# The framework's timeline scheduler in place of its default for a two-block stack on one core

## The chip, the cores and the metric

The kernel runs on one core of a Trainium2 chip. The metric is the device time of one execution in microseconds; the median of three runs of the kernel before is 1540.05 us (1540.02 to 1541.18).

The engines are named as in the profile: PE multiplies matrices (PEld is its weight load), DVE is the vector engine, ACT the scalar engine, POOL the general one, and SP issues the transfers (SPq is its queue). Each takes its instructions in the order of its own list and waits at an instruction until the operands are there.

## The reference

256 tokens of width 1024 pass through two blocks. All matrices are float32 in HBM. The first block has two layers, each a mixer and an MLP with modulated norms; the second has three mixers side by side, a cross attention to 256 memory tokens and a gated feed-forward:

```python
for layer in range(2):                                   # first_block
    sh1, sc1, g1, sh2, sc2, g2 = split(silu(c) @ ada_w[layer] + ada_b[layer], 6)
    h = rmsnorm(x, norm_g[layer, 0]) * (1 + sc1) + sh1
    mixed = ssd_na_mixer(h, ...) if layer == 0 else mlstm_mixer(h, ...)
    x = x + g1 * rmsnorm(mixed, norm_g[layer, 1])
    h = rmsnorm(x, norm_g[layer, 2]) * (1 + sc2) + sh2
    x = x + g2 * rmsnorm(square(relu(h @ mlp_w1[layer])) @ mlp_w2[layer], norm_g[layer, 3])

fq, fk, fv, ff, su, hq, hf, hi, hg, gl = split(rmsnorm(x, norm_mix) @ w_in)   # second_block
gates = sigmoid(gl)
merged = (gates[0] * (fox_attention(fq, fk, fv, ff) @ wb[0])
          + gates[1] * (s5_mixer(su) @ wb[1])            # scan, gelu, then gated by z @ w_glu
          + gates[2] * (hgrn2_mixer(hq, hf, hi, hg) @ wb[2]))
x = x + merged @ w_out
x = x + cross_attention(rmsnorm(x), rmsnorm(mem), ...)
x = x + swiglu(rmsnorm(x), w_gate_up, w_down)
```

`ssd_na_mixer` is a two-way state-space scan (SSD) and a neighbourhood attention of 16 heads, joined by one output matrix.

## The kernel before

The weights are streamed from HBM in units of 1 MB: `unit` (L431) loads one into a tile `raw` (3 buffers), ACT rounds each half to a high part `wh` (L351), and DVE subtracts it for the low part `wl` (L360); there are 4 buffers of each, so two units at a time. Every product is three matmuls on high and low parts (L366). A projection unit is 48 matmuls with 256 columns, one of an output matrix 24 with 512. Transposes run on PE as well (L370). PSUM has eight banks, shared between the tags `mm` (projections) and `ax` (all else), four and four, five and three in the second block's mixer.

`stack_kernel` (L1863) writes the stages one after the other. The stretches of the trace are: the start, to 44 us, where the modulation vectors are made on DVE from 1 MB units of `ada` (L635) while the first tokens are normed; the projections of `mixer0`, 44 to 218; its eight output units and what goes with them, 218 to 283; the norm into the first MLP, to 295; first MLP, mLSTM mixer, second MLP, to 950; `mixer2`, 950 to 1280; `cross`, to 1345; `ffn`, to the end.

In `mixer0` (L968) M0_ORDER, "aaaxxxaaaxbzaaazaaazz", gives the order of 21 steps: `a` projects queries, keys or values of four heads, `x` and `z` belong to the scan. After every third `a` the heads of a column c are queued as a generator (`na_heads`), which makes two pairs of heads, each with its bias tables `nb` (L1100): scores into `ax`, a reduction on DVE that adds the table (L1109, `nam`), exponentials on ACT, transposes on PE, and the product with the values from the tile `smp`. `tick` runs a step of a queued generator between the units. `out_units` then sums eight output units in four accumulators (here `mm_2649` to `mm_2652`), in the order of M0_ROWS, the four of the attention first.

Into the MLP, `mem_fill` puts projections of the memory (`mm_3127`, `mm_3186`, in fwh and fwl tiles) where PE would wait for the norm; `order` (L885) asks that the first of them be issued ahead of the norm's transposes.

In `mixer2` (L1650) M2_ORDER, "su fox hz hv g2 g0 b0 glu dr g1 b1 b2", names projections, gates (`g`), branch products (`b`) and the S5 gate (`glu`); the S5 scan (tiles s5w, su, s5c) is a background generator and the HGRN scan (xn, hS, hb) a queued one, in levels: xn on DVE, products on PE, a predicated copy into hS on DVE (L1513).

The code so far gives an order of creation and the data dependencies. The framework's scheduler makes the list of each engine from it: it simulates the program and puts next what it takes for ready. The first argument of `TileContext` is the device; the mode of that simulation is an option of it.

## Time and profile before

| | before |
|---|---|
| median of the runs | 1540.05 us |
| profiled execution | 1534.84 us |
| its span | 1533.0 us |
| mean granted clock of PE | 0.991 |
| PE busy | 1472.9 us (96%) |
| DVE busy | 1164.9 us (76%) |
| ACT busy | 854.5 us (56%) |

The rows further down come from this one execution, whose time is its span and 1.8 us around it. PE's matmuls overlap in the records: one is shown with 0.28 us where the next starts 0.12 us later, so the pace is read from rows that group many of them.

### The profile page before, as it was taken

How to read it: one execution, taken by the hardware profiler on the slowest of the kernel's cores; microseconds unless marked ns; L12 is line 12 of the kernel's file. 1: busy time of each engine (PE TensorE's matmuls, PEld its weight loads, DVE VectorE, ACT ScalarE, POOL GpSimd, SP SyncE). 2: the span in 40 equal slices, each digit the busy share in tenths (PEclk: the TensorE clock that was granted, in tenths of full speed). 3: DMA queues.
4: the chain of work that ended last, by engine and by line, in shares of the span. 5: the costliest groups of instructions: out<-in, count | busy, mean ns of one | idle time of the engine just before them, and what ended most of it. 6: DMA issues, size and time to landing. Idle time of an engine off the chain costs nothing.

```text
span 1533.0 us, 25395 instructions
## 1 busy us (share of the span) xinstructions
PE 1472.9 (96%) x9964; PEld 1318.1 (86%) x9964; DVE 1164.9 (76%) x2223; ACT 854.5 (56%) x1502; POOL 4.5 (0%) x24
## 2 busy tenths in 40 slices
PE   2998999999999899999999999999999999999999
PEld 2887887888988899998889889877789998799998
DVE  7788988877778886657988866867798987565555
ACT  4786774654456555545756765445444457444443
POOL 0000000000000000000000000000000000000000
PEclk8999999999999999999999999999999999999999
DMA  9755887587875894446676664323333365245542
GB/s 347 258 166 171 293 300 275 185 308 289 319 296 187 300 297 152 166 145 221 232 246 242 232 226 187 133 95 131 130 132 135 114 227 199 97 141 189 193 178 98
DMA packets 62058, 315.47 MB, mean 206 GB/s; under 512 B 6385, under 2 KB 15217, under 8 KB 28146
## 3 DMA queue, kind: packets, MB, share of 16 engines
q1 hardware_dynamic: 61938, 313.85, 57.6%
q8 instruction: 78, 1.28, 0.3%
q14 instruction: 42, 0.34, 0.1%
HBM read 304.77 MB, written 9.05 MB: 205 GB/s over the span
## 4 chain that ended last, share of the span: by engine, by line
PE 77%; DVE 12%; DMA 5%; ACT 5%; issue 2%; SPq 0%; ACTq 0%; DVEq 0%
PE mm L366 50%; PE ax L366 24%; DVE wl L360 3%; PE ax L370 2%; DMA bp<-cs_d 1%; ACT xn L351 1%; ACT wh L351 1%; DMA raw<-in_ada 1%; DVE acc L751 1%; ACT nb L351 1%; DMA grow<-in_rows 1%; DVE acc L638 1%; DMA raw<-in_wts 1%; DMA bp<-nM_d 1%; PE mm L370 0%
## 5 line engine op out<-in xcount | busy, mean ns | idle before, releaser
L360 DVE TENSOR_TENSOR wl<-raw,wh 128x1024 fp32r<-128x1024 f32 x400 | 485.9, 1223 | 204.6 <-ACT wh L351 203.2
L351 ACT ACTIVATE wh<-raw 128x1024 fp32r<-128x1024 f32 x400 | 419.4, 1057 | 372.0 <-PE mm L366 212.2
L366 PE MATMUL mm<-xh,wh 128*128 128x256 f32 x1536 | 441.4, 287 | 6.1 <-ACT bp L351 3.1
L366 PE MATMUL mm<-xh,wl 128*128 128x256 f32 x1536 | 439.3, 286 | 2.5 <-DVE wl L360 2.5
L366 PE MATMUL mm<-xl,wh 128*128 128x256 f32 x1536 | 438.8, 286 | 0.0
L366 PEld LDWEIGHTS mm<-xh,wh 128*128 128x128 f32 x1536 | 295.9, 193 | 15.2 <-issue 5.6
L366 PEld LDWEIGHTS mm<-xh,wl 128*128 128x128 f32 x1536 | 295.9, 193 | 7.5 <-DVE wl L360 3.7
L366 PEld LDWEIGHTS mm<-xl,wh 128*128 128x128 f32 x1536 | 296.0, 193 | 5.6 <-issue 3.8
L366 PE MATMUL mm<-wh,xh 128*128 128x256 f32 x496 | 143.9, 290 | 0.0
L366 PE MATMUL mm<-wl,xh 128*128 128x256 f32 x496 | 143.2, 289 | 0.5 <-DVE wl L360 0.5
L366 PE MATMUL mm<-wh,xl 128*128 128x256 f32 x496 | 142.0, 286 | 0.0
L366 PE MATMUL ax<-wh,mhh 128*128 128x512 f32 x256 | 102.5, 400 | 0.0
L366 PE MATMUL ax<-wh,mhl 128*128 128x512 f32 x256 | 101.4, 396 | 0.0
L366 PE MATMUL ax<-wl,mhh 128*128 128x512 f32 x256 | 101.4, 396 | 0.0
L366 PEld LDWEIGHTS mm<-wl,xh 128*128 128x128 f32 x496 | 96.0, 194 | 4.9 <-issue 2.3
L366 PEld LDWEIGHTS mm<-wh,xh 128*128 128x128 f32 x496 | 95.8, 193 | 2.2 <-issue 1.7
L366 PEld LDWEIGHTS mm<-wh,xl 128*128 128x128 f32 x496 | 95.9, 193 | 1.2 <-issue 1.1
L366 PEld LDWEIGHTS ax<-wh,mhl 128*128 128x128 f32 x256 | 48.2, 188 | 11.9 <-DVE mhl L360 0.4
L366 PEld LDWEIGHTS ax<-wh,mhh 128*128 128x128 f32 x256 | 48.3, 189 | 10.6 <-ACT wh L351 0.5
L366 PEld LDWEIGHTS ax<-wl,mhh 128*128 128x128 f32 x256 | 48.2, 188 | 10.6 <-issue 0.2
L751 DVE CUSTOM_DVE_ANT_0 acc<-raw,crow 128x1024 f32<-128x1024 f32 x32 | 39.0, 1219 | 3.0 <-DMA raw<-in_ada 2.7
L363 DVE SCALAR_TENSOR_TENSOR acc<-raw,cond,acc 128x1024 f32<-128x1024 f32 x28 | 35.8, 1278 | 6.5 <-DMA raw<-in_ada 6.2
(486 smaller groups left out, 2574.5 us busy)
## 6 DMA issues: line engine op xcount, KB each, us to landing
raw<-in_wts SPq DMA_DIRECT2D x214, 1024.0 KB, 4.9
raw<-in_ada SPq DMA_DIRECT2D x48, 1024.0 KB, 5.8
nb<-in_nab SPq DMA_DIRECT2D x16, 256.0 KB, 5.0
grow<-in_rows SPq DMA_DIRECT2D x16, 256.0 KB, 6.1
bp<-cs_d SPq DMA_DIRECT2D x16, 256.0 KB, 5.5
s5tab<-s5t SPq DMA_DIRECT2D x16, 256.0 KB, 2.7
s5tl<-s5tab SPq DMA_DIRECT2D x16, 256.0 KB, 3.6
meml<-mem_d SPq DMA_DIRECT2D x2, 1024.0 KB, 5.3
```

The source lines that it names most:

```text
L351: return self.nc.scalar.activation(out=out, in_=in_, func=func, **kw)
L360: return self.nc.vector.tensor_tensor(out=out, in0=in0, in1=in1, op=op)
L363: return self.nc.vector.scalar_tensor_tensor(out=out, in0=in0, scalar=s, in1=in1, op0=op0, op1=op1)
L366: return self.nc.tensor.matmul(out, lhsT, rhs, start=start, stop=stop)
L370: return self.nc.tensor.transpose(out, in_, self.ident[0:k, 0:k])
L638: nc.vector.tensor_tensor_reduce(out=acc, in0=raw[:, k * D:(k + 1) * D], in1=self.crow, scale=1.0, scalar=0.0, op0=ALU.mult, op1=ALU.add, ...
L751: nc.vector.tensor_tensor_reduce(out=acc, in0=w, in1=self.crow, scale=1.0, scalar=0.0, op0=ALU.mult, op1=ALU.add, accum_out=s8[:, j:j + 1])
```

## The change

The scheduler is asked for its other mode, which keeps a timeline of the engines while it chooses. Nothing else is edited; every engine has the same instructions as before (9,528 matmuls, 2,223 rows on DVE, 1,366 activations, 400 transfers), and POOL has them in the same order.

```diff
-    with tile.TileContext(nc) as tc:
+    with tile.TileContext(nc, schedule_with_timeline_sim=True) as tc:
         stack_kernel(tc, aps)
```

On SP, at the start of the program, right after the first tokens (raw from in_ada are modulation units, nf a small weight, cst masks, nb attention tables, mem the memory tokens, raw from in_wts weight units; + is the place after the change):

```order
 L635 DMA raw_196<-in_ada 128x2048
+L461 DMA nf_244<-in_wsm 128x512
+L1878 DMA cst_80<-in_cst 128x512
+L1100 DMA nb_689<-in_nab 128x512
+L1100 DMA nb_692<-in_nab 128x512
+L1100 DMA nb_822<-in_nab 128x512
+L978 DMA crow_d_90<-G0_86 1x1024
+L1100 DMA nb_825<-in_nab 128x512
+L847 DMA mem_1674<-in_mem 128x1024
 L635 DMA raw_201<-in_ada 128x2048
 L438 DMA raw_222<-in_wts 128x2048
 L438 DMA raw_232<-in_wts 128x2048
```

Eight small transfers moved ahead of the second modulation unit; two tiles of gain rows, grow, moved in the same way, behind raw_289.

On PE, a pair of attention heads in `mixer0`; before, next to projections (ax_2385 is the product with the values, ax_2434 and ax_2437 the scores of the following pair, mm_2464 a projection):

```order
L366 MATMUL mm_2464<-xl_109,wh_2467 128x256
L366 MATMUL ax_2385<-smp_2426,nv_2381 64x256
L366 MATMUL ax_2385<-smp_2410,nv_2381 64x256
L366 MATMUL ax_2385<-smp_2426,nv_2381 64x256
L366 MATMUL ax_2385<-smp_2410,nv_2381 64x256
L366 MATMUL ax_2437<-nk_2312,nq_2244 128x256
L366 MATMUL ax_2434<-nk_2312,nq_2244 128x256
L366 MATMUL ax_2437<-nk_2312,nq_2244 128x256
L366 MATMUL ax_2434<-nk_2312,nq_2244 128x256
L366 MATMUL mm_2464<-xh_108,wl_2468 128x256
```

And on PE now, behind all projections, the pair before those two (ax_2016 the product with the values, ax_2065 and ax_2068 its scores and their transposes):

```order
L366 MATMUL ax_2068<-nk_1872,nq_1735 128x256
L366 MATMUL ax_2065<-nk_1872,nq_1735 128x256
L366 MATMUL ax_2068<-nk_1872,nq_1735 128x256
L366 MATMUL ax_2065<-nk_1872,nq_1735 128x256
L366 MATMUL ax_2391<-nk_2312,nq_2244 128x256 x2
L370 MATMUL ax_2065<-cst_80,nb_2063 128x128 x4
L370 MATMUL ax_2068<-cst_80,nb_2066 128x128 x4
L366 MATMUL ax_2388<-nk_2312,nq_2244 128x256 x2
L366 MATMUL ax_2016<-smp_2173,nv_2012 64x256
L366 MATMUL ax_2016<-smp_2087,nv_2012 64x256
L366 MATMUL ax_2016<-smp_2173,nv_2012 64x256
L366 MATMUL ax_2016<-smp_2087,nv_2012 64x256
```

The last four of the eight pairs moved behind the last projection, among the output units, and between the scores of this one and its product stand only the scores of the next.

On DVE, in `mixer2` between the splits of two gate units, before (wl_12932 and wl_12936 are one unit, wl_12993 the first half of the next):

```order
L360 TENSOR_TENSOR wl_12932<-raw_12929,wh_12931 128x1024
L360 TENSOR_TENSOR wl_12936<-raw_12929,wh_12935 128x1024
L357 TENSOR_SCALAR s5w1_12524<-s5w1_12524 128x512
L360 TENSOR_TENSOR xn_12763<-xn_12763,hq_10267 128x64x8
L360 TENSOR_TENSOR s5w1_12524<-s5w1_12524,su0_10329 128x512
L360 TENSOR_TENSOR wl_12993<-raw_12990,wh_12992 128x1024
```

And now, the last twelve of the 64 rows from wl_12936 to wl_12993 (s5c_12523 is the operand of the glu product):

```order
L360 TENSOR_TENSOR su1_10390<-su1_10390,s5w2_12533 128x512
L360 TENSOR_TENSOR xn_12797<-xn_12797,hq_10267 128x256x2
L360 TENSOR_TENSOR s5c_12523<-su1_10390,s5bt_12522 128x512
L1513 COPY_PREDICATED hS0_12255<-G0_86,ax_12802 128x512
L1513 COPY_PREDICATED hS1_12257<-G0_86,ax_12808 128x512
L360 TENSOR_TENSOR xn_12814<-hb_12172,hz_10266 128x512
L360 TENSOR_TENSOR xn_12814<-hb_12172 128x512
L360 TENSOR_TENSOR xn_12814<-xn_12814,hq_10267 128x512
L357 TENSOR_SCALAR s5w1_12524<-s5w1_12524 128x512
L360 TENSOR_TENSOR s5w1_12524<-s5w1_12524,su0_10329 128x512
L1513 COPY_PREDICATED hS0_12255<-G0_86,ax_12819 128x512
L360 TENSOR_TENSOR wl_12993<-raw_12990,wh_12992 128x1024
```

Three rows stood between these two units, 62 stand there now: the end of the S5 scan and six levels of the HGRN scan, which were spread over the units before.

Into the first MLP, PE's list before has the four groups of transposes of the norm at the start of mm_3186 and behind its 18th and 25th matmul (two, one, one); now all 48 matmuls of mm_3186 come first and the four groups behind them.

## Rows read from the trace of the kernel before

**Rows 1.** The page: busy time of an engine; the chain that ended last.
```profile
PE 1472.9 (96%) x9964; PEld 1318.1 (86%) x9964; DVE 1164.9 (76%) x2223; ACT 854.5 (56%) x1502; POOL 4.5 (0%) x24
...
PE 77%; DVE 12%; DMA 5%; ACT 5%; issue 2%; SPq 0%; ACTq 0%; DVEq 0%
```

**Rows 2.** Windows: stretch, length, busy time (instructions) by engine, clock, DMA share, GB/s.
```profile
44.00:218.00 174.00, 161.75 (x1228) 142.96 (x1227) 148.33 (x349) 129.20 (x289) 0.00 (x0) 0.97 0.70 232
218.00:283.00 65.00, 64.55 (x328) 52.69 (x325) 56.83 (x98) 35.59 (x58) 0.00 (x0) 1.00 0.74 268
...
950.00:1174.00 224.00, 222.15 (x1497) 181.14 (x1496) 176.86 (x341) 100.75 (x168) 1.08 (x2) 1.00 0.37 128
1174.00:1224.00 50.00, 49.46 (x416) 48.86 (x416) 46.51 (x80) 25.89 (x34) 0.00 (x0) 1.00 0.36 127
```

**Rows 3.** Timeline of SP's queue: start, length, what is issued.
```profile
4.62 6.66 SPq L635 DMA_DIRECT2D raw<-in_ada  x2
13.48 7.08 SPq L438 DMA_DIRECT2D raw<-in_wts  x2
```

**Rows 4.** Windows of the start, and the sizes of transfers in the first 50 us.
```profile
2.00:18.00 16.00, 2.02 (x10) 1.97 (x11) 10.87 (x43) 6.49 (x17) 0.00 (x0) 1.00 1.02 392
...
20.00:22.00 2.00, 0.00 (x0) 0.00 (x0) 1.66 (x7) 2.00 (x5) 0.00 (x0) 1.00 0.43 74
...
nb<-in_nab SPq DMA_DIRECT2D x4, 256.0 KB, 6.1
mem<-in_mem SPq DMA_DIRECT2D x1, 512.0 KB
```

**Rows 5.** Timeline of DVE, end of the start: start, length, operation, idle before.
```profile
43.97 2.36 DVE L360 TENSOR_TENSOR wl<-raw,wh 128x1024 fp32r<-128x1024 f32 x2 [0.26 <-ACT wh L351]
```

**Rows 6.** Timelines of PE and DVE: one pair of attention heads, and the next.
```profile
148.76 0.38 PE L366 MATMUL ax<-nk,nq 64*128 64x256 f32 x1
...
156.05 1.08 PE L366 MATMUL ax<-smp,nv 128*64 128x256 f32 x8
...
149.50 0.42 DVE L1109 CUSTOM_DVE_ANT_0 nb<-ax,nb 128x256 f32<-128x256 f32 x1
...
158.99 0.41 DVE L1109 CUSTOM_DVE_ANT_0 nb<-ax,nb 128x256 f32<-128x256 f32 x1
```

**Rows 7.** The chain that ended last, in the first MLP: start, length, what.
```profile
307.14 5.60 PE ax L366 x24
313.18 5.75 PE mm L366 x48
```

**Rows 8.** Timeline of PE at a stall, and windows behind it.
```profile
122.66 1.97 PE L366 MATMUL ax<-qt,xt 128*64 128x256 f32 x8 [4.09 <-DVE qt L360]
...
122.00:124.00 2.00, 1.34 (x8) 0.77 (x8) 1.74 (x2) 0.52 (x1) 0.00 (x0) 0.50 0.54 103
...
126.00:128.00 2.00, 2.00 (x11) 2.00 (x11) 1.15 (x4) 0.10 (x1) 0.00 (x0) 0.50 0.44 175
```

**Rows 9.** Timeline of PE into the first MLP: last transposes, first projection that waited.
```profile
290.22 0.65 PE L370 MATMUL mm<-cst,xn 128*128 128x128 f32 x4
...
295.00 0.39 PE L366 MATMUL mm<-xh,wh 128*128 128x256 f32 x1 [1.14 <-ACT wh L351]
```

**Rows 10.** The second block's mixer: timeline of PE at mm_12633; two pieces of the chain.
```profile
1174.31 0.37 PE L366 MATMUL mm<-fyh,wh 128*128 128x256 f32 x1
...
1163.19 3.63 PE ax L366 x24
...
1198.64 1.90 PE mm L366 x16
```

**Rows 11.** The same mixer: timeline of DVE, rows of the HGRN scan.
```profile
1189.06 0.72 DVE L1513 COPY_PREDICATED hS<-G,ax 128x512 f32<-128x512 int32 x1
1189.68 0.68 DVE L360 TENSOR_TENSOR xn<-hb,hz 128x512 f32<-128x512 f32 x1
1190.28 0.69 DVE L360 TENSOR_TENSOR xn<-hb 128x512 f32<-128x512 f32 x1
```

## The prediction

> **What bounds the kernel now.** I read the page first, then the busy time by stage, then the timeline where a stage is not full of TensorE work. The page shows PE busy for 96% of the span and PE on 77% of the chain that ended last [rows 1]: the kernel is as long as PE's work plus the moments in which PE has nothing to do. The stages differ. From 44 to 218 us (the 22 projections of the first mixer) PE is busy 161.75 of 174 us while DVE is busy 148.33; from 1174 to 1224 PE is busy 49.46 of 50 and DVE 46.51; from 950 to 1174 PE is busy 222.15 of 224 [rows 2]. So an order that keeps all the work can gain at most the idle time (12.25 us in the first mixer, some 13 us of DMA-bound start, next to nothing later), while it can lose wherever DVE, which has 3.5 us of air in 50 around 1200 us, is given its work at the wrong time. The question for each stage is whether PE still finds ready operands.
>
> **The change, place by place.** The instructions are the same on every engine; each engine works through its list in order, so work that another engine's list has put late is late for PE too. I compared the two lists and gave each row the duration that the trace of before has for the same instruction; "so much less done" below is the sum of the rows that the new list has moved behind a point. The MLPs, the mLSTM mixer, the cross attention and the feed-forward keep their order of weight units, or move rows by a few us where PE is full; I take them as nothing, and 1 us each way in the range.
>
> *Start.* The first 44 us wait for DMA: from 2 to 18 us the queue moves 392 GB/s, about 0.4 MB a us, and only at 20 to 22 us does it fall to 74 GB/s [rows 4], where it waits for a raw buffer. The new list of SP puts nf, cst, crow, four neighbourhood tables (256 KB each) and the 512 KB of mem ahead of the second of the two modulation units that before went out together at 4.62 us [rows 3, 4]. Of that, nf, cst and crow came before the first projection unit anyway; what is new ahead of it is the four tables, mem and two tiles of gain rows (grow), 1.0 + 0.5 + 0.5 = 2.0 MB, or 5 us at 0.4 MB a us. The hole at 20 to 22 us can take back some 1.5 us of it. The first split of a weight unit for the projections, at 43.97 us [rows 5], would come 3.5 us later; PE's later waits in the mixer may hide a little of this. I take +3, bounds 0 (all hidden) and +5 (no hole filled).
>
> *First mixer, projections.* The new order runs more projections before the first attention and splits weight units earlier on DVE; by the last projection DVE has done 11 us less, ACT 22 us less and PE 10 us less than before, all of it attention and scan work put behind. PE waits less for splits as long as that lasts: of the 12.25 us idle I take two thirds back, -8, bounds 0 and -12.
>
> *First mixer, tail.* What was put behind comes due with the eight out-projection units. Before, the last of the eight pairs of attention heads is done inside the last projection; now four pairs stand behind it, and from the third out unit on the matmuls need their results. One pair is a chain over PE, DVE and ACT: its scores are on PE at 148.76 us, DVE reads them at 149.50, the product with the values runs at 156.05 to 157.13 us, and the next pair's DVE part starts at 158.99 [rows 6]. From scores to product it is 8.4 us and from pair to pair 9.5. In the new PE list the first of the four pairs has one out unit of 24 matmuls (5.60 us [rows 7]) between scores and product, the second only the next pair's scores, the third 24 matmuls again, the fourth a handful of normalisation matmuls, some 1.5 us. Four chains of 8.4 us are 33.6; scores of the third run beside the second, about 2.5 us off; cover 5.6 + 5.6 + 1.5 = 12.7. PE waits 33.6 - 2.5 - 12.7 = 18 us. Softmax work of different pairs may overlap more than I see, so I take +15, bounds +8 (only the second and fourth wait, 4 us each) and +22 (9.5 us a pair, less overlap).
>
> *Into the first MLP.* Before, 30 of the 48 matmuls of the second memory filler stand between groups of transposes of the normed tokens, and 23 stand behind the last group; with them in place PE still waits 1.14 us for the first projection [rows 9]. Now all 48 come first and all four groups of transposes follow, with nothing behind. 48 matmuls take 5.75 us [rows 7], so 23 are 2.8 us of cover gone, and the 1.14 stays: +3, bounds +1 (the transposes start sooner) and +4. The same pattern is at the end of the second MLP, with fewer matmuls: +1.
>
> *The mixer of the second block.* Here the list of DVE puts the end of the S5 scan and six levels of the HGRN scan behind the unit splits of the branch and gate projections. Up to the projection mm_12633, which started at 1174.31 us, DVE has 32 us less done, PE 48 matmuls of the scans less. 24 of such matmuls take 3.63 us [rows 10], so PE comes there 7.3 us earlier, at 1167, and is through with it and its twin, 48 matmuls, at 1172.8. But DVE's row merged3 waits for that, and behind it, before the second half of the glu operand (s5c from su1), now stand 52 rows of the scans, and the split wl_12993 some nine rows later. On this stretch a row follows the one before every 0.60 to 0.63 us [rows 11]; a fifth of the 52 rows are shorter ones, so 52 rows are about 31 us without any wait, 36 with the busy times instead of the spacing. The operand is there at 1204 to 1209. PE's list still has 34 glu matmuls, 33 of mm_12928 and 16 small ones in front of mm_12989, about 10 us, which therefore starts at 1214 to 1219 instead of 1198.64 plus some tenths, where the rows of before have it [rows 10]. That is 15 to 20 us. After it both lists have the same work left and DVE is lighter, but PE was full there before, so nothing comes back. I take +14, since PE can spread some of the waiting matmuls; bounds +5 and +20.
>
> **A clock cost on top.** In this trace PE sat idle for 4.09 us ahead of 122.66 us, and from 122 to 128 us it ran at a granted clock of 0.50, 1.2 GHz instead of 2.4 [rows 8]: a long stall is followed by some us at half speed, and a matmul of 1.2 GHz takes twice its time, so a stall costs up to 3 us more than its length. I count it in the range, not in the sum, since most matmuls right behind these stalls are followed by another wait. The Trainium skill, TensorE: Matmul & The Clock Gate, section Loop structure matters more than you think, says the same as a rule: matmuls have to stay back to back, and a long wait makes the array run cold. Rows 8 agree; by that rule the sum would be some 6 us higher.
>
> **The sum.** Against the profiled execution of 1534.84 us (span 1533.0): start +3, projections -8, tail +15, norm gaps +3 and +1, second mixer +14, together +28, or 1563. The median of the runs is 1540.05, 5.2 us or 0.34% above the profiled one; on that scale 1563 is 1568.
>
> **Rivals.**
> - *The stalls come, with the clock behind them.* Each of the four pair waits and the wait for s5c is followed by half speed, and the bounds at the upper end hold: 1568 + 6 for the clock + 7 for the tail + 6 for the mixer, 1575 to 1587. For it: rows 8. Against: the cover in the tail gets slower too and then hides nothing that is lost.
> - *The early splits win.* This ends on the other side, faster. The place is the projections of the first mixer: if DVE, busy 148.33 of 174 us, is what keeps PE waiting there, the whole 12 us come back; if the four pairs then overlap so far that only 4 us of wait is left in the tail, and DVE's 52 rows in the second mixer start before merged3's wait is over, so that 2 us are lost, the sum is 3 - 12 + 4 + 1 + 2 = -2, or -6 with the start and the norm gap hidden: 1534 to 1538. It decides by whether the pair-to-pair time without projections around it falls below 5 us; the 8.4 us within a pair speak against, as do the rows in order on DVE.
> - *No difference.* The same work on a PE that is 96% busy, gains at the projections equal to the losses: 1540, when the tail costs 8 and the mixer 1. The point is the same as above.
> - *PE is not really full.* The weight loads (PEld) are busy 181.14 of 224 us where PE is busy 222.15 [rows 2]. If that difference were air, a better order could press up to a fifth out of this stretch, and with 13 us of it the time would be 1555. The Trainium skill, Perfetto Trace Analysis, section Identifying the Most-Contended Engine, holds matmul busy time for a poor measure and weight-load time for a better one. Against: where PE does nothing but back-to-back matmuls of one form, it keeps their pace, 5.75 us for 48 [rows 7], and there too weight loads are not all of it; so I give it 3 in 100.
>
> **How the numbers follow.** Forecast near 1568 (1555 to 1575) 52 in 100; stalls with the clock (1575 to 1592) 20; a smaller loss (1544 to 1555, among it the fourth rival), 10; no difference 6; faster 12. The likeliest gives 1568. The range must hold 8 in 10: from 1546, which leaves out the two cases at or under 1543 (18 in 100), up to 1592. A measurement of this kernel can tell about 0.2%, 3 us, from no change; by the cases, slower 0.82, within it 0.06, faster 0.12.
>
> **What would show it.** In the new profile: the first split of a projection unit after 46 us instead of 43.97 (start); PE's busy share from there to the last projection over 0.93 (projections); PE waits of several us for nb or smp among the out units, and that stage over 75 us instead of 65 (tail); a wait for wh or xh of 3 to 5 us at the first matmul of the first MLP; in the second block a wait of PE of 10 us or more for s5c with DVE busy without a break. The prediction is wrong if the out units run without waits, which means that a pair is no chain of 8.4 us when alone, or if the glu matmuls find s5c ready, which means that DVE went through the scan rows before the PE work that I took to hold it.

## The result, and the profile after

The changed kernel takes 1606.87 us (median of 4 runs, 1605.35 to 1609.24), the kernel before 1540.32 on the same chip: a ratio of 1.043, 95% interval 1.041 to 1.045. It is slower, as forecast, but by 66.5 us and not by 28: beyond the upper end of the range. The profiled execution took 1606.95 us, with a span of 1605.2 instead of 1533.0.

The page of the changed kernel answers to [rows 1]: first the busy time of the engines, then the engines' shares of the chain that ended last.

```profile
PE 1499.5 (93%) x9964; PEld 1339.2 (83%) x9964; DVE 1161.5 (72%) x2223; ACT 853.2 (53%) x1502; POOL 4.5 (0%) x24
...
PE 77%; DVE 9%; DMA 8%; ACT 4%; issue 2%; SPq 0%; ACTq 0%; DVEq 0%
```

DVE and ACT are busy 3.4 and 1.3 us less than before. PE has the same 9,964 records, and they took 26.6 us more; the other 45.6 us of the 72.2 are idle time of PE. So two things cost: PE waits more, and its matmuls take longer.

To see where, I cut both traces at the same matmuls, those with which a stage begins. The cuts are at 54.80 and 297.30 us in the changed kernel where they are at 50.20 and 279.60 in the one before, and so on. A stretch then has nearly the same work in both; only 20 records have passed from the mLSTM mixer to its output units. Windows of the kernel before (stretch, length, busy us and records of PE, PEld, DVE, ACT and POOL, granted clock, DMA share, GB/s), for the first mixer, the norm into the first MLP, the mLSTM mixer's output units with the norm into the second MLP, and the second block's mixer:

```profile
50.20:279.60 229.40, 216.71 (x1471) 186.05 (x1471) 198.57 (x427) 159.59 (x338) 0.00 (x0) 0.98 0.70 235
279.60:318.80 39.20, 37.72 (x290) 36.04 (x289) 32.27 (x77) 25.58 (x55) 0.00 (x0) 1.00 0.57 209
...
645.60:761.20 115.60, 113.91 (x718) 102.54 (x717) 86.54 (x211) 66.53 (x133) 0.53 (x1) 1.00 0.53 191
...
937.50:1247.20 309.70, 307.31 (x2207) 265.61 (x2206) 249.02 (x451) 144.81 (x222) 2.07 (x4) 1.00 0.38 134
```

The same four of the changed kernel, and behind them the cross attention:

```profile
54.80:297.30 242.50, 222.61 (x1471) 187.98 (x1471) 194.53 (x415) 157.43 (x334) 0.00 (x0) 0.94 0.65 219
297.30:342.70 45.40, 40.49 (x289) 38.23 (x288) 33.81 (x88) 27.04 (x59) 0.00 (x0) 0.92 0.47 169
...
671.00:801.60 130.60, 121.58 (x738) 108.68 (x737) 93.83 (x237) 72.57 (x148) 0.53 (x1) 0.96 0.48 170
...
981.00:1308.40 327.40, 313.22 (x2207) 271.15 (x2206) 249.42 (x450) 143.31 (x220) 2.07 (x4) 0.97 0.37 128
1308.40:1424.00 115.60, 105.77 (x607) 92.50 (x607) 72.13 (x173) 62.00 (x136) 0.00 (x0) 0.96 0.43 157
```

In the first mixer the same 1,471 records of PE took 5.9 us longer, and PE's idle time (length less busy time) rose from 12.7 to 19.9 us; the two make up the 13.1 us. All stretches, read in the same way:

| stretch of the kernel before, us | longer by | forecast | PE idle before, after |
|---|---|---|---|
| start, to 50.2 | +4.6 | +3 | 28.9, 31.7 |
| first mixer, to 279.6 (projections −15.6, output units +28.7) | +13.1 | +7 | 12.7, 19.9 |
| into the first MLP, to 318.8 | +6.2 | +3 | 1.5, 4.9 |
| first MLP, to 469.2 | 0.0 | 0 | 0, 0 |
| its norm and the mLSTM mixer, to 645.6 | +1.5 | 0 | 6.1, 9.2 |
| output units of that mixer, into the second MLP, to 761.2 | +15.0 | 0 | 1.7, 9.0 |
| second MLP, to 937.5 | +3.1 | +1 | 1.0, 3.2 |
| second block's mixer, to its first output unit, 1247.2 | +17.7 | +14 | 2.4, 14.2 |
| its output units, cross attention, to 1351.8 | +11.0 | 0 | 2.1, 9.8 |
| feed-forward, to the end | 0.0 | 0 | 3.7, 3.8 |

The stretches in which weights stream through a full PE, the first MLP and the feed-forward, are as long as before to a tenth of a us. All that was lost stands in the mixers and at the places where one stage hands over to the next.

**The start.** The timeline of DVE has the first split of a projection unit at 47.81 us, against 43.97 [rows 5]:

```profile
47.81 2.36 DVE L360 TENSOR_TENSOR wl<-raw,wh 128x1024 fp32r<-128x1024 f32 x2 [0.26 <-PE mm L366]
```

**The first mixer's output units.** The timeline of PE (start, length, operation, idle before and what ended it) and two windows show the pairs of heads that were put off, to be held against the pair in [rows 6]:

```profile
231.24 0.84 PE L370 MATMUL ax<-cst,nb 128*128 128x128 f32 x4 [0.97 <-ACT nb L351]
233.94 1.12 PE L370 MATMUL ax<-cst,nb 128*128 128x128 f32 x4 [1.85 <-ACT nb L351]
235.74 1.98 PE L366 MATMUL ax<-smp,nv 128*64 128x256 f32 x8 [0.69 <-ACT smp L351]
242.76 1.92 PE L370 MATMUL ax<-cst,nb 128*128 128x128 f32 x8 [2.05 <-ACT nb L351]
246.61 1.98 PE L366 MATMUL ax<-smp,nv 128*64 128x256 f32 x8
258.16 1.08 PE L366 MATMUL ax<-smp,nv 128*64 128x256 f32 x8
267.45 1.08 PE L366 MATMUL ax<-smp,nv 128*64 128x256 f32 x8
...
235.00:240.00 5.00, 4.32 (x19) 2.72 (x19) 0.23 (x1) 0.60 (x1) 0.00 (x0) 0.51 1.01 408
...
245.00:250.00 5.00, 3.87 (x14) 1.83 (x13) 1.80 (x10) 3.12 (x12) 0.00 (x0) 0.50 0.28 101
```

The waits are for exponentials (`nb`) and for normalised products (`smp`), as the forecast said, but none is longer than 2.05 us. Behind them the granted clock is 0.50, 1.2 GHz, and the product of 8 matmuls takes 1.98 us instead of 1.08 [rows 6]. The four products follow one another after 10.9, 11.5 and 9.3 us, against 9.5 from pair to pair in the kernel before.

**The second block's mixer.** The chain that ended last (start, length, what) behind the row `merged3`, shortened to where engines change:

```profile
1208.26 0.60 DVE merged L363
1208.85 1.20 DVE s5w L360 x2
...
1214.31 5.48 PE ax L366 x16
1219.81 0.73 DVE hS L1513
1220.54 1.17 DVE xn L360 x2
...
1230.07 5.51 PE ax L366 x24
1235.60 0.73 DVE hS L1513
1236.33 1.17 DVE xn L360 x2
...
1238.85 2.74 PE ax L366 x16
```

It is DVE's block of scan rows that the forecast saw, but it doesn't run through: every level of the HGRN scan needs matmuls that stand alone on PE, and these run slowly, 24 in 5.51 us where [rows 10] has 24 in 3.63. The window around the first of them:

```profile
1210.00:1215.00 5.00, 2.74 (x10) 2.14 (x11) 5.00 (x11) 0.00 (x0) 0.00 (x0) 0.50 0.43 180
```

DVE is busy for the whole of it, PE for half, at the lower of its two clocks.

**A place the forecast had passed over: how a stage ends.** In the kernel before the last two output units of a stage run the first 128 tokens and then the other 128, so two of the four accumulators are whole some 7 us ahead of the others, and the norm's first half is hidden. First before, then after, ACT's first read of the accumulators behind the mLSTM mixer:

```profile
715.26 0.60 ACT L351 ACTIVATE xn<-mm 128x512 f32<-128x512 f32 x1 [0.93 <-PE mm L366]
...
751.27 0.60 ACT L351 ACTIVATE xn<-mm 128x512 f32<-128x512 f32 x1 [0.43 <-PE mm L366]
```

Before, these units go on for another 6.5 us behind 715.26, to 721.8. After, the second half can be read 1.15 us behind the first (at 752.42), so nothing covers the norm, and PE waits. The memory filler that was meant to cover it needs a PSUM bank which the norm still has to empty. Its first matmul in the changed kernel, here and at the end of the first MLP:

```profile
509.35 0.46 PE L366 MATMUL ax<-fwh,memh 128*128 128x256 f32 x1 [4.41 <-DVE x L363]
...
757.40 0.55 PE L366 MATMUL mm<-fwh,memh 128*128 128x256 f32 x1 [5.47 <-DVE x L363]
```

The six stages end in the kernel before with 6.8 to 7.0 us between the first and the last accumulator; in the changed one with 0.7 to 2.8.

### The profile page after: what moved, and what is told of

It is laid out like the page before. It is cut to its first block, busy times and chain, and to the rows that moved or that the text cites. A ratio compares the mean times of both kernels' runs of the same rounds, so it can differ in the third digit from the quotient of the medians.

```text
span 1605.2 us, 25434 instructions
## 1 busy us (share of the span) xinstructions
PE 1499.5 (93%) x9964; PEld 1339.2 (83%) x9964; DVE 1161.5 (72%) x2223; ACT 853.2 (53%) x1502; POOL 4.5 (0%) x24
## 4 chain that ended last, share of the span: by engine, by line
PE 77%; DVE 9%; DMA 8%; ACT 4%; issue 2%; SPq 0%; ACTq 0%; DVEq 0%
PE mm L366 51%; PE ax L366 24%; DMA raw<-in_wts 5%; DVE wl L360 2%; ACT wh L351 2%; PE ax L370 2%; DMA raw<-in_ada 1%; DVE fwl L360 1%; ACT nb L351 1%; DMA bp<-nM_d 1%; DMA bp<-cs_d 1%; DVE acc L638 0%; DMA grow<-in_rows 0%; DVE acc L751 0%; ACT nf L351 0%
## 5 line engine op out<-in xcount | busy, mean ns | idle before, releaser
L366 PEld LDWEIGHTS mm<-xh,wl 128*128 128x128 f32 x1536 | 297.7, 194 | 14.2 <-DVE wl L360 8.0
L366 PEld LDWEIGHTS ax<-wh,mhh 128*128 128x128 f32 x256 | 48.7, 190 | 13.2 <-ACT mhh L351 2.4
L351 ACT ACTIVATE xn<-xn 128x128 f32<-128x128 f32 (+3 forms) x44 | 24.6, 577 | 35.2 <-DVE xn L360 27.2
```

Of the source, the lines that this page charges most:

```text
L351: return self.nc.scalar.activation(out=out, in_=in_, func=func, **kw)
L366: return self.nc.tensor.matmul(out, lhsT, rhs, start=start, stop=stop)
```

## The experiments

Three theories stood against one another: that the lost stagger of the accumulators makes the loss (S); that displaced scan, attention and norm work does, each at its own place (D); and, later, that the order of the transfers does (T). The figures in brackets are ratios to the kernel before with their 95% intervals. The us that came "back" are differences between medians of four occasions, on which the kernel before had 1540.32, 1539.82, 1538.96 and 1538.08 us, so they are good to about 2 us. Changes of a stage are read at the cuts of the table, in one profiled execution of each kernel.

**e1, the stagger given back.** The changed kernel; only in a stage's last units the second half's matmuls are asked to come behind the first half's:

```diff
         for t in range(2):
-            for i, (_, yh, yl) in enumerate(units):
-                self.down_half(...)
+            with self.tc.issue_after(self.last_pe.ins) if t and last else nullcontext():
+                for i, (_, yh, yl) in enumerate(units):
+                    self.down_half(...)
```

> The changed kernel, with one thing put back: in the last output units of every stage the matmuls of the second token half are issued behind those of the first, so that the accumulators of tokens 0 to 127 end some 6 us ahead of the others, as before the change. Theory S (the part of the loss that the forecast missed lies at the stage boundaries, where the four accumulators now end within 1 to 3 us of each other and the norm and the fillers have nothing to run beside): 25 to 35 us of the 66 come back, 1572 to 1582 us, and the gaps ahead of the first filler out of the mLSTM mixer (5.5 us) and into the MLPs close. Theory D (the loss is all in work put off inside the two large mixers): 0 to 6 us, 1601 to 1607.

Measured 1598.46 us (1.038, 1.035 to 1.040): 8.4 us back, between the two. In the profiled execution, 4.5 us faster than that median, the way into the first MLP gained 3.1 us on the changed kernel, the end of the mLSTM mixer 1.5, the way out of the second MLP 2.1, and the cross attention with the end of the mixer before it 6.8. The chain behind the mLSTM mixer shows why it is so little:

```profile
748.35 0.70 ACT xn L351 x2
...
751.24 0.68 DVE x L363
752.05 8.49 PE mm L366 x48
```

The first half is read earlier, but the rows of the norm still come one behind the other on ACT and DVE, and PE stands for 3.74 us ahead of 752.05. The edit is not the stagger alone, either: the scheduler simulates anew, and inside the mLSTM mixer all three engines' lists are no longer those of the changed kernel.

**e2, the stagger taken from the kernel before.**

```diff
+            for part in (0, 1) if last else ((0, 1),):
+                for t in range(2):
+                    self.down_half(ws[i], yh, yl, acc, t, f, l, part)
```

> The kernel before, default scheduler, with one thing taken over: the matmuls of a stage's last output units go through both token halves in turn, so that all four accumulators end together. Theory S: 20 to 35 us slower, 1560 to 1575. Theory D: within 5 us of before, 1540 to 1545.

Measured 1561.46 us (1.014, 1.011 to 1.017): 21.6 us lost, as theory S expected, 3.6 on average at each of six ends. In the profile the loss stands behind the ends: 2.5, 2.7, 4.0 and 5.1 us behind the first four, 7.1 behind the last two together. The timeline of PE shows the same wait as in the changed kernel, at a place where the kernel before has none:

```profile
732.25 0.58 PE L366 MATMUL mm<-fwh,memh 128*128 128x256 f32 x1 [3.39 <-DVE x L363]
```

So in the kernel before the stagger is worth as much as a third of the loss, and giving it back on one engine isn't enough. That the norm's rows on the others have to be in step with it fits e1's chain; no run changes those rows alone.

**e5, e6 and e8, one mixer each in its order of before.** These are the changed kernel with one stage (its norm included) held to the order of before on PE, DVE and ACT. The same edit stands around `mixer2` (e5), `mixer0` (e6) and `mixer1`, the mLSTM mixer (e8):

```diff
+def as_listed(tc, rows):
+    made = {i.name: i for i in rows}
+    for names in ROWS:                      # the list of before, an engine at a time
+        last = None
+        for n in names:
+            i = made.get(n)
+            if i is not None:
+                if last is not None:
+                    tc.add_manual_dep(i, last.name, NOSYNC, reason="listed order")
+                last = i
...
+    lo0 = len(tc.nc.cur_bb.bb.instructions)
     with S.phase("mixer2", 5, LATE2):
...
+    as_listed(tc, list(tc.nc.cur_bb.bb.instructions)[lo0:])
```

> The changed kernel, but all that is created in the second block's mixer and its norm (PE, DVE, ACT) is issued in the order of the kernel before, by order-only dependencies; the rest stays with the timeline scheduler. From the two traces this stage with the step into the next cost 18 us in the mixer and 5 at its exit. Theory D: 15 to 25 us come back, 1582 to 1592, and the glu product no longer waits for s5c. Rival (its loss is a loss of PE clock and transfers around it, which stay): under 6 us, 1601 to 1607.

Measured 1586.63 us (1.031, 1.029 to 1.033): 20.2 us back, within the range of theory D. The stage is 4.5 us longer than before instead of 17.7, and the block of scan rows is gone. That is 13.2 us in place; another 5.3 came back in the norm and the mLSTM mixer, whose lists the edit leaves as they were. The same lists took 177.9 us there in the changed kernel, 176.3 in e4, 180.5 in e6 and 172.6 in e5, where the clock was 1.00 instead of 0.97. So the figure of a stage from one execution can move by several us without any edit to it, and in place the edit gave less than the 15 us expected. The stretch in which the changed kernel had the chain above is now:

```profile
1214.00:1240.00 26.00, 26.00 (x222) 25.87 (x222) 25.27 (x38) 14.35 (x20) 0.00 (x0) 1.00 0.32 111
```

PE is full at a clock of 1.00 beside a full DVE.

> The changed kernel, but all that is created in the first mixer and its norm (PE, DVE, ACT) is issued in the order of the kernel before. From the two traces the projections gained 16 us, the out units lost 29 and the step into the first MLP 6. Theory D (gain and loss are one thing, attention put off): both go, net 15 to 20 us come back, 1587 to 1592. Rival (the projections' gain is a thing of its own): the projections gain stays in the rest and only the transfers change, under 6 us.

Measured 1593.88 us (1.034, 1.032 to 1.037): 13.0 us back, 2 short of what theory D expected. From the first projection to the last the stage is 0.6 us longer than before and its output units 0.7, instead of −15.6 and +28.7: the gain and the loss go together. The windows' row of the output units has 1.1 us of idle time left:

```profile
224.40:284.00 59.60, 58.50 (x280) 46.86 (x280) 51.92 (x78) 33.60 (x50) 0.00 (x0) 1.00 0.72 264
```

> The changed kernel, but all that is created in the mLSTM mixer and its norm is issued in the order of the kernel before (PE, DVE, ACT). From the two traces its out units with the step into the second MLP cost 10.4 us and the MLP's first units 4.5; with the accumulators alone put back (e1) 1.8 of the 10.4 came back. Theory D (the heads of this mixer are put off too, so that the last out units wait for them): the out units are back to before, 9 to 14 us less, 1593 to 1598. Rival (the accumulators' common end is all of it): 2 to 4 us less, 1603 to 1605.

Measured 1599.72 us (1.039, 1.037 to 1.042): 7.2 us back, between the two theories. In place it is clear, the output units of the mLSTM mixer lose 0.0 us instead of 10; but from the end of the first MLP to these units the trace is now 7.3 us longer than before instead of 1.5, and the second MLP's beginning is still 4.0 late. Of the 7.3, 3.4 stand at the step out of the first MLP, which the edit leaves in the new order, and 3.9 in the beginning of the listed mixer; why those is not shown.

**e9, all three mixers and the cross attention.** The same edit around all of them.

> The changed kernel, with the three mixers and the cross attention in the order of before on PE, DVE and ACT; the start, both MLPs and the feed-forward stay as the timeline scheduler has them. If the parts add up: 72 us of the trace less 13 (first mixer), 6 and 5 (the steps around it), 14 (mLSTM mixer and its exit), 18 and 11 (second mixer to feed-forward) leaves 5 to 10, 1545 to 1550. If the parts only shift waits to other places: 1560 or more.

Measured 1563.92 us (1.016, 1.013 to 1.019): 43.0 us back. The three alone gave 20.2, 13.0 and 7.2, together 40.4, but here the cross attention is listed too, and in the profile its stretch is 1.5 us longer than before instead of 11.0. So the whole is some 7 us less than the sum of its parts. The time is above what was expected if the parts add up, and in the range of the rival: what is left, 25 us, is the start (3.9 in the profile), the norms into the first MLP and the mLSTM mixer (4.5 and 3.4), and 2.6 to 3.7 us each inside the beginning of that mixer, into the second MLP, out of it, and in the beginning of the third mixer.

**e7, every stage but the last listed, the transfers left.** PE, DVE and ACT have the order of before from the start to the cross attention; SP has the timeline mode's.

> The changed kernel, with everything from the start to the cross attention issued on PE, DVE and ACT in the order of the kernel before; the transfers on SP stay in the timeline scheduler's order, and the feed-forward is free. Theory D (work put off on the compute engines is all of the loss, but for the start): 1540 + 4.6 us of the start, 1543 to 1548. Rival T (the order of the transfers is itself a large part, since the chain of the changed kernel has 5% of weight loads where the one of before had 1%): 1555 or more.

Measured 1551.1 us (1.008, 1.005 to 1.011): 55.8 us of the loss is the order on the three computing engines, 12 are left, and up to the feed-forward only SP's list still differs. In the profile, 16.3 us longer than that of before, the largest are the start (4.6), the stretch of the mLSTM mixer (2.9) and the second block's mixer (4.5); no other is over 1.8. Neither theory had it alone: the median is between D's figure and T's.

**e12, all that had helped, together.** Three mixers listed, the stagger of e1, and SP in its order of before through the start and the first mixer.

> The changed kernel with all known parts put back at once: the three mixers in the order of before on PE, DVE and ACT, the transfers of the start and the first mixer in the order of before on SP, and the accumulators of the last output units one token half after the other. What is left to the timeline scheduler is the MLPs' steps, the cross attention, the feed-forward and later transfers. If the ledger holds: e9 (1564) less 4 to 5 of the start and 4 to 8 of the accumulators at the MLPs' ends, 1551 to 1556. If causes overlap: 1557 or more. Below 1540 only if the timeline scheduler's order is better where it is left free.

Measured 1556.24 us (1.011, 1.008 to 1.014). It is at the upper end of what the ledger gave. The start is 0.6 us ahead of before, where e9 has it 3.9 late, so its loss was SP's order. The rest, 18 us, is spread in the profile over the steps into the first MLP (3.8) and the second (3.7), the norm and the mLSTM mixer (5.3), the cross attention (3.3) and smaller ones. Into the first MLP e7, with the norms' rows listed as well, loses only 0.3. Nothing of the new order that I kept has beaten the kernel before.

**e3 and e4, a narrower cure that failed.** The changed kernel, in which only the splits of weight units are kept behind DVE rows written earlier, in the first mixer (e3) and in the second block's (e4), so that units are not split ahead of old scan and attention work:

```diff
-                self.tt(l, src, h, ALU.subtract)
+                (self.tc.keep_in_program_order if self.pin else id)(self.tt(l, src, h, ALU.subtract))
...
+        S.pin = True; acc = S.mixer0(...); S.pin = False
```

> The changed kernel, with one rule added in the first mixer: the DVE row that splits a weight unit is issued behind all DVE rows written ahead of it in the program, so no split overtakes attention or scan work; all else stays free. Theory D (splits that overtake the side work on DVE are how the attention ends up in the tail): the four pairs are back among the projections, the tail is 25 us or more shorter, the projections some 10 to 20 longer; net 0 to 15 less, 1592 to 1607. Rival (the tail comes from PE's or ACT's own order): tail and time as in the changed kernel, within 3 us.

> The same rule in the second block's mixer alone. Theory D: no block of scan rows stands before the glu operand any more, the stretch from mm_12633 to the second half of glu is under 15 us where the changed kernel has 50, but the rule is stricter than the order of before and puts scan rows ahead of splits, so some of the time comes back earlier in the mixer: 1588 to 1602 (the full order of before gave 1587). Rival: the block stays, 1604 to 1610.

Measured 1646.28 us (1.070, 1.066 to 1.074) and 1711.21 us (1.112, 1.109 to 1.115). Both theories missed: each is much slower than the changed kernel. The windows of the two stages:

```profile
48.00:260.00 212.00, 153.82 (x1069) 133.88 (x1067) 134.62 (x311) 115.30 (x251) 0.00 (x0) 0.81 0.45 147
...
981.00:1270.00 289.00, 236.41 (x1389) 183.74 (x1388) 168.53 (x324) 97.76 (x163) 1.69 (x4) 0.84 0.28 96
```

PE is idle for 58 and 53 us of them, at a mean clock of 0.81 and 0.84: now the units wait behind scan and attention rows that wait themselves. In e3 the output units did get shorter, by 18.1 us, but the projections 73.5 us longer. In e4 the block ahead of the glu operand is gone (the glu product starts 1.8 us behind the projections ahead of it, where the changed kernel takes 36.6), but those projections end 115 us later in the stage. The edit is too strict to tell the theories apart; it only shows that keeping every split behind the older rows is worse than letting it overtake them.

## Why the prediction was right in sign and wrong in size

*That it is slower, and why.* An order that keeps the work can gain only PE's idle time and can lose wherever ready operands run out: that held. PE's busy share fell from 96 to 93%. (The start's "some 13 us" of idle time stand in no row; the table has 28.9.)

*Start, +3 against +4.6.* Right in mechanism (e12 takes it back with SP's order) and within its bounds, at the upper end. The hole was filled, as assumed: from 20 to 22 us the changed kernel moves 438 GB/s where it was 74. The first split comes 3.8 us later, close to the 3.5 that the text worked out; the half us that it took off for later waits is not there, since PE is 4.6 us late at the table's cut.

*Projections, −8 against −15.6.* Outside its bound of −12. The bound was the idle time; but some of PE's own work was put off as well, and that shortens the stretch without being a gain. Between the first and the last projection PE has 1,107 records where it had 1,195 (windows as above; first before, with the output units behind it, then the projections of the changed kernel):

```profile
50.20:220.60 170.40, 158.15 (x1195) 139.10 (x1195) 147.39 (x353) 126.07 (x288) 0.00 (x0) 0.97 0.69 226
220.60:279.60 59.00, 58.55 (x278) 46.95 (x277) 51.18 (x75) 33.52 (x51) 0.00 (x0) 1.00 0.72 261
...
54.80:209.60 154.80, 143.17 (x1107) 129.74 (x1107) 136.13 (x301) 106.46 (x230) 0.00 (x0) 0.97 0.69 222
```

Idle time is 11.6 us, against 12.25 before: so the gain that was forecast, waits taken back, hardly came about at all. I had read the shorter stretch as both. The 10 us less PE work that the text itself counts, 15.0 as measured, should have gone into the tail in full.

*Output units, +15 against +28.7.* Right in kind: the waits are for `nb` and `smp`, between pairs whose cover is gone. The put-off records come back here (366 instead of 278): PE is busy for 20.9 us more, and that is most of it. PE's idle time in the stretch is 8.3 us, about half of the 15 that I had summed for it:

```profile
209.60:297.30 87.70, 79.44 (x366) 58.23 (x365) 58.40 (x115) 50.98 (x106) 0.00 (x0) 0.90 0.59 214
```

Projections and output units have to be taken together: forecast +7, measured +13.1, of which 7.2 is idle time and 5.9 longer records of PE, at a granted clock of 0.94 instead of 0.98. The clock is just what the sum had left out. The Trainium skill, TensorE: Matmul & The Clock Gate, section Loop structure matters more than you think, has PE go cold, to the lower clock, where a long wait stands ahead of every matmul, and the prediction gave 6 us for it. The traces agree that it goes cold and make it dearer: it did so behind waits of 2.05 us and less, too, and PE's records took 26.6 us longer in all.

*Into the first MLP, +3 against +6.2.* The wait is about as foreseen, the rest was not. PE's idle time in the stretch rose by 3.4 us, most of it at the first projection of the MLP, for 4.02 us where it was 1.14:

```profile
314.76 0.45 PE L366 MATMUL mm<-xh,wh 128*128 128x256 f32 x1 [4.02 <-ACT wh L351]
```

The other 2.8 us are longer records of PE, at a clock of 0.92 over the stretch. Nor is the order of the transposes the whole cause of the wait: e1, which changes the accumulators' order, gets 3.1 us of the 6.2 back, with waits of 1.6 and 1.4 us left there.

*"I take them as nothing": the step that failed.* The mLSTM mixer and the cross attention, with the norms around them, were given 1 us each way. They lost 1.5 + 15.0 and 11.0 us, and the second MLP's 3.1 stands against 1. That is 30.6 us of the 72.2, where the forecast has 1, and most of what it fell short by. I had looked whether the weight units keep their order, and they do; I had not looked at the order inside the last two units, halves of tokens, on which the hiding of the norm rests. It was to be seen in the two lists. e2 shows that the kernel before loses 21.6 us without it, and e8 that the mLSTM mixer's output units lose nothing once its own lists are back, though 5.8 us more are lost ahead of them. How the 30.6 us divide between the stagger and the other rows is not shown: of these stretches e1, with the stagger on PE, gets 10.2 back.

*The second block's mixer, +14 against +17.7.* The best step in size. DVE's rows do stand ahead of the glu operand, and mm_12989 starts 16.6 us later against the stage's begin; 15 to 20 was worked out. The way there was different. PE came to mm_12633 20.8 us earlier, not 7.3, since 95 of its records were put off and not 48. Behind it, the stretch to mm_12989 is 37.4 us longer, where the put-off matmuls run in a chain with DVE, in part at half the clock (before, up to mm_12633; then the changed kernel, up to it and behind it):

```profile
937.50:1174.30 236.80, 234.95 (x1604) 193.94 (x1603) 183.60 (x348) 108.21 (x176) 2.07 (x4) 1.00 0.39 135
...
981.00:1197.00 216.00, 216.00 (x1509) 183.34 (x1508) 155.53 (x296) 102.17 (x168) 2.07 (x4) 1.00 0.41 144
1197.00:1247.00 50.00, 38.11 (x219) 29.29 (x218) 45.22 (x77) 12.44 (x16) 0.00 (x0) 0.83 0.18 58
```

The sign that the prediction named for it, one wait of PE of 10 us or more for s5c, did not come: the longest wait there is 3.29 us, for the HGRN scan's xn, and the 11.9 us of idle time are made of six of them. The named waits "of several us" among the output units were of 2 us as well.

*The rivals.* "The stalls come, with the clock behind them" (1575 to 1592) was nearest, 15 us short, and had 20 in 100; it is what happened, at more stages than it named. "PE is not really full" was right in a small part of its premise: before mm_12633 the 1,509 records of the changed kernel took 0.143 us each on PE, against 0.146 for the 1,604 of before (234.95 us), while the weight loads took 0.12 us each in both. By these figures 5 us of a PE that looked full were air. Part of that is the mix of shapes: at the pace that each shape has in the trace of before, the put-off records are worth 16.0 us, which leaves about 3. The Trainium skill, Perfetto Trace Analysis, section Identifying the Most-Contended Engine, on matmul busy time as the poorer measure, agrees with these rows in kind. The early splits didn't win: e6 shows that the shorter projections and the longer tail are one thing.

*What stays open.* The 12 us of the transfers' order (e7) are placed only in part, 4.6 at the start and 7.4 in the stretches of two mixers out of 16.3 in the profile, and only the start was undone. How much of the longer matmuls is clock, and how much queueing inside PE, no run separated, but the traces allow an estimate. Behind the start the granted clock stood at 0.50 for 88.8 us of the changed kernel, with PE busy for 76.6 of them, and for 13.7 us of the kernel before, with PE busy for 12.7. If all that work took twice its time, it is 32 us more, and PE's records took 24.8 us more there: the clock alone is enough to account for them.

## What to carry to other kernels

When only the order changes, go through the ends of the stages first: who finishes first among the accumulators, which rows that lets run early, and which bank they set free. Work put off on a full engine is no gain in the stretch that it leaves; count it again, at the lower clock, in the stretch where it comes due and has nothing beside it. And an order that was good on one engine need not be good beside other lists on the rest: given back on PE alone the stagger returned 8.4 us; taken from the kernel before, it cost 21.6.

## What was not expected of the hardware

- The lower clock came behind short waits: in the first mixer's output units no wait that the timeline names is over 2.05 us, and yet the granted clock is 0.51 and 0.50 in the windows at 235 and 245 us. Over the kernel the same 9,964 PE records took 1.8% longer.
- A PE that the records show busy for 216.00 of 216 us had done some 3 us more work, counted by shapes, than the kernel before did in the same busy time.
- The order of the transfers on one queue, with the same bytes and all three computing engines in their order of before, cost 12 us, 0.8% (0.5 to 1.1, e7).
